# Streaming encoder step: new keys inside the cached keys' products, stick-breaking low halves on VectorE, and one rotary projection for all four query heads

## The chip, the cores and the metric

The kernel runs on one core of a Trainium2 chip. Each core has five engines with instruction streams of their own: PE (TensorE: matmuls and weight loads), DVE (VectorE), ACT (ScalarE), POOL (GpSimd) and SP (SyncE, which issues the DMAs here). They meet through semaphores. The metric is the time of one execution on the device in microseconds (us) (lower is better).

## The reference, cut to what matters

Two layers run over a prompt of 512 frames and over 8 running streams of 16 frames each (the sample, 128 rows in all). A layer projects its input, mixes it by three branches, and ends with an output projection, a layer norm, a squared-ReLU MLP and another layer norm. The change touches two branches: latent attention (MLA, 4 heads, with a rotary part of 64 per head) and stick-breaking attention (SB, 4 heads of 64).

```python
# both attentions of the sample see 1024 cached keys and 16 new ones of their own stream
ckv_all = jnp.concatenate([ckv_p, ckv], 1)
k_all   = jnp.concatenate([k_p, kc], 1)
# MLA
q = jnp.einsum('bsc,chd->bshd', rms_norm(b_cq, g_cq), w_uq)     # 384 -> 4 heads x (128 + 64)
q_rope = rope(q[..., NOPE_DIM:], q_pos)
scores = (einsum('bqhc,bkc->bhqk', q_lat, ckv) + einsum('bqhr,bkr->bhqk', q_rope, krope)) * MLA_SCALE
p = softmax(where(visible, scores, -inf)); out = einsum('bhqk,bkc->bqhc', p, ckv)
# SB
z = einsum('bqhd,bkhd->bhqk', q, k) * SB_SCALE
log_skip = where(mask, log_sigmoid(-z), 0)
w = where(mask, exp(log_sigmoid(z) + suffix_sum(log_skip)), 0); out = einsum('bhqk,bkhd->bqhd', w, v)
```

Everything is float32. The kernel splits each operand into a high part in the matmul's format (fp32r) and a low rest, and sums two or three products for each one of the reference.

## The kernel before, in words

Two streams of work are written as generators and woven together: P (the prompt) and S (the sample), whose steps of one layer are the preparation of queries and new keys (`s_prep`), the MLA over the caches (`lane_smla`), the SB over the caches (`lane_ssb`), and output and MLP (`s_out_mlp`). All instructions are recorded first; `Plan.schedule` then sets the order of every engine's instructions with a list scheduler (costs per instruction, tile slots, the rank of each instruction), and `Plan.follow` fixes that order. Every compute instruction is issued in one helper, so the profile shows them all at line 417 and all DMAs at line 433; they are told apart by the names of their tiles.

**Operands.** `split(hi, lo, src)` makes a high half with an ACT copy and a low half with a subtraction, on DVE unless an engine is given. For the caches of both attentions that engine is POOL (`KLO = VLO = pool`): tile `cT` holds a block of 512 cached keys (raw block `rawK`), `cN` a block of values (`rawV`).

**Scores of the sample** (`sample_scores`). The streams go in four pairs `pr`, two streams `j` each. For each stream there are two blocks `c` of 512 cached keys, each over two halves `ct` of the contraction, high and low: four matmuls of 512 columns into one PSUM bank (five in MLA, with the rotary part `kr`). The stationary operand holds high and low queries of 4 heads and 16 frames, so rows 64 to 127 of the result are added to rows 0 to 63 (`fold_to`: an ACT copy to `tmp`, a DVE addition). The new keys are a product of their own, `fresh`: four (MLA: five) matmuls of 128 columns, against the new keys of all 8 streams, of which a mask leaves 16. The banks are `x` (two) for SB and `sC` (three) for MLA and `fresh`.

**Values of the sample** (`weights_T`, `sample_values`). The 1152 weights of a pair (1024 cached, 128 new) are transposed in nine blocks of 128 to `pTs`, and are the stationary operands of matmuls with `cN`, 256 columns each; the ninth block multiplies the new values `cnh` or `vn`.

**Prompt's queries in MLA** (`lane_pmla`). The heads go in two pairs `a`, the frames in two halves `tp`. For each `(a, tp)`, `q_rope` projects the rotary part in 18 matmuls of 128 columns (bank `acc`, read `acc<-w,cqT`) and rotates it with five DVE instructions, and `q_nope` projects the rest in 18 matmuls of 256 columns (`acc<-cqT,w`). The weights come from `w_uq` in two loads for each `a`.

```python
            split(c4[:, 0], c4[:, 1], raw, KLO)
...
        def fresh(j, q, s_):
            for ct in range(2):
                pe.matmul(s_[:, :128], q[ct], new[:, 0, ct], start=(ct == 0), stop=False)
                pe.matmul(s_[:, :128], q[ct], new[:, 1, ct], start=False, stop=(ct == 1 and kr_new is None))
```

Of the kernel before, what the change touches and what calls it, by code (L numbers as in the profile page):

```python
# [20 lines left out]
L = 2  # L21
# [4 lines left out]
H = 4  # L26
# [70 lines left out]
class Plan:  # L97
# [111 lines left out]
    def schedule(self, prio):  # L209
# [32 lines left out]
        block = {name: len(v) for name, v in under.items()}  # L242
        opens = {}
# [42 lines left out]
        def issue(k, e, s):  # L286
# [18 lines left out]
            for name in o["tiles"]:  # L305
                left[name] -= 1
                if not left[name]:
# [9 lines left out]
                    grant(t)  # L317
            for x in succ[k]:
# [180 lines left out]
def hybrid_step(  # L499
# [5 lines left out]
    t_x, t_ckv, t_sbk, t_kr, t_ckvv, t_sbv, t_ws, t_wss, t_bs, t_bss, t_wukT, t_wkv, t_win, t_wout, t_wup,  # L505
# [27 lines left out]
    VLO = KLO = pool  # L533
# [123 lines left out]
    junk = cp.tile([128, 512], BF16, name="junk")  # L657

    def rms_to(out, src, g, n):
        ss = little([128, 1], F32, "ss")  # L660
        act.activation(junk[:, :n], src, AF.Square, accum_out=ss)
        r = rstd_of(ss, 1.0 / n, 1)
        dve.scalar_tensor_tensor(out, src, r[:, 0:1], g, ALU.mult, ALU.mult)
# [19 lines left out]
    def rope_apply(out, src, rope, t, pl, nh):  # L683
        t1 = pl.tile([128, nh, 64], F32, tag="rp1", name="rp1")
# [359 lines left out]
    def lane_pmla(l):  # L1044
# [5 lines left out]
        gmx = bcast(g_mix[l, 256:768], 512, mq, "gmxb")  # L1050
        W, KN, VM, CQ, CK, QR, QT, QX, PP = {}, {}, {}, {}, {}, {}, {}, {}, {}

        def q_tr(a, tp):

            if tp == 0:
                W[a] = load_wq(l, a), load_wkv(l, a, mp)
# [57 lines left out]
        def q_rope(a, tp):  # L1114
            cT, wq = CQ[a, tp], W[a][0]
            yield at("acc", cT, wq[2][1])
            pa = bank("acc")
            for i in range(2):
                c = slice(i * 128, (i + 1) * 128)
                o = pa[:, i * 128:(i + 1) * 128].rearrange("p (h d) -> p h d", h=2)  # L1120
                for k in range(3):
                    wh, wl = (x.rearrange("p (h d) -> p h d", h=2)[:, :, NOPE:] for x in wq[k])
                    mm3(o, cT[:, 0, k, c], cT[:, 1, k, c], wh, wl, k == 0, k == 2)
            qr = mp.tile([128, 4, 64], F32, tag="qr", name="qr")
            t = 2 * tp
            src = pa[:, :256].rearrange("p (t h d) -> p t h d", t=2, h=2)
            t2 = mp.tile([128, 4, 64], F32, tag="rp2", name="rp2")
            for i in range(2):
                hs = slice(2 * i, 2 * i + 2)
                cc = rope[:, 0, t + i].unsqueeze(1).to_broadcast([128, 2, 64])  # L1130
                ssn = rope[:, 1, t + i].rearrange("p (a b) -> p a b", a=2).unsqueeze(1).to_broadcast([128, 2, 2, 32])
                dve.tensor_tensor(qr[:, hs], src[:, i], cc, ALU.mult)
                sw = src[:, i].rearrange("p h (a b) -> p h a b", a=2)[:, :, ::-1, :]
                dve.tensor_tensor(t2[:, hs].rearrange("p h (a b) -> p h a b", a=2), sw, ssn, ALU.mult)
            dve.tensor_tensor(qr, qr, t2, ALU.add)
            qd = QR[a, tp] = mp.tile([128, 4, 2, 64], F32R, tag="d2", name="qd1")
            split(qd[:, :, 0], qd[:, :, 1], qr)

        def q_nope(a, tp):
            cT, wq = CQ.pop((a, tp)), W[a][0]  # L1140
            yield at("acc", cT)
            pa = bank("acc")
            for h in range(2):
                c = slice(h * 192, h * 192 + NOPE)
                for k in range(3):
                    mm3(pa[:, h * 256:(h + 1) * 256], wq[k][0][:, c], wq[k][1][:, c], cT[:, 0, k], cT[:, 1, k], k == 0, k == 2)
# [42 lines left out]
        late = []  # L1189

        def p_st(a, qt):
            nk = (qt + 1) * 128
            pp, r = PP.pop((a, qt))
# [14 lines left out]
        def p_v(a, qt, j, hs, pT, r):  # L1208
# [15 lines left out]
            if hs[-1] == 1:  # L1224
                if a == 1:
                    rms_to(xy[:, t, 512:1024], xy[:, t, 512:1024], gmx, 512)
# [199 lines left out]
    def weights_T(pl, p):  # L1426
        pTs = pl.tile([128, 9, 2, 2, 64], F32R, tag="pTs", name="pTs")
        for c0 in range(0, 9, 4):
            n = min(4, 9 - c0)
            yield at("sC", p)  # L1430
            pt = bank("sC")
            for i in range(n):
                tr(pt[:, i * 128:(i + 1) * 128], p[:, (c0 + i) * 128:(c0 + i + 1) * 128])
            split(pTs[:, c0:c0 + n, :, 0], pTs[:, c0:c0 + n, :, 1],
                  pt[:, :n * 128].rearrange("p (i j c) -> p i j c", j=2, c=64))
        return pTs

    def sample_scores(pl, s2, src, q_of, new, msk, n, kr_of=None, kr_new=None):
# [5 lines left out]
        def run(f):  # L1444
            return at("none" if f.args[3] else acc, *(x for x in f.args[4:] if x is not None))

        def block(j, q, c, ct, c4, kr):
            if ct == 0:
                held.append(bank(acc))
            s_ = held[0]  # L1450
            pe.matmul(s_, q[ct], c4[:, 0], start=(ct == 0), stop=False)
            pe.matmul(s_, q[ct], c4[:, 1], start=False, stop=(ct == 1 and kr is None))
            if ct:
                if kr is not None:
                    pe.matmul(s_, q[2], kr, start=False, stop=True)
                fold_to(s2[64 * j:64 * j + 64, 512 * c:512 * c + 512], held.pop(), 512, pl)

        def fresh(j, q, s_):
            for ct in range(2):
                pe.matmul(s_[:, :128], q[ct], new[:, 0, ct], start=(ct == 0), stop=False)  # L1460
# [441 lines left out]
```

## Time and profile before

| | |
|---|---|
| median of 3 runs | 1744.52 us (1735.86 to 1745.47) |
| the profiled execution's own time | 1738.5 us |
| its span, first to last instruction | 1736.6 us |
| instructions | 24320 |
| PE busy | 1665.9 us, 96% of the span, 8756 matmuls |
| DVE busy | 1167.8 us, 67% |
| ACT busy | 1017.5 us, 59% |
| POOL busy | 461.8 us, 27% |
| mean granted TensorE clock | 0.988 |
| DMA | 305.05 MB, mean 176 GB/s |

The profile is a page on one execution. A row such as `L417 PE MATMUL sC<-cT,qlT 128*128 128x512 f32 x128` reads: line 417, PE, bank `sC` written from moving operand `cT` and stationary operand `qlT`, array of 128 by 128, result of 128 partitions by 512 columns, 128 times. A matmul's shown duration holds its way through the array, so durations of neighbours overlap; what one costs in a dense stretch is read from start to start.

### The profile page before, as it was taken

Reading aid. Unit: us, or ns where it says so; the run is one execution under the profiler, and the core shown is the slowest. Engines: PE = TensorE matmul, PEld = TensorE weight load, DVE = VectorE, ACT = ScalarE, POOL = GpSimd, SP = SyncE. Lnnn points to the kernel's source line nnn. Section 1 sums busy time; section 2 is a strip of 40 time slices with the busy share of each in tenths; the row PEclk is TensorE's granted clock in tenths of the full one; section 3 lists DMA queues with packets and bytes.
Section 4 is the critical chain, followed back from the end, with each engine's and each line's share of the span. In section 5 each row is a group of like instructions: output and inputs, shape, how many; then the busy total and the mean of one; then the engine's idle time right before and its main releaser. Section 6 shows DMA issues by size and latency. Waiting matters only on the chain.

```text
span 1736.6 us, 24320 instructions
## 1 busy us (share of the span) xinstructions
PE 1665.9 (96%) x8756; PEld 1404.2 (81%) x8756; DVE 1167.8 (67%) x1592; ACT 1017.5 (59%) x1891; POOL 461.8 (27%) x320
## 2 busy tenths in 40 slices
PE   8999999899998999999999989999999999999998
PEld 6898988787886778888878988888778778788886
DVE  3487776846675587666744876868467766776766
ACT  4586785546664556463335857855467656564632
POOL 0000446534664300000000004466446552000000
PEclk9999999999999999999999999999999999999999
DMA  7236565445444587674353255665465456875732
GB/s 260 92 97 184 184 186 197 157 151 186 158 153 133 182 274 251 204 246 141 130 165 105 91 170 171 197 217 170 142 184 168 134 154 232 265 246 191 252 125 84
DMA packets 145817, 305.05 MB, mean 176 GB/s; under 512 B 32032, under 2 KB 46496, under 8 KB 145696
## 3 DMA queue, kind: packets, MB, share of 16 engines
q1 hardware_dynamic: 145696, 303.49, 54.2%
q8 instruction: 69, 1.13, 0.3%
q14 instruction: 52, 0.43, 0.1%
HBM read 286.14 MB, written 17.30 MB: 175 GB/s over the span
## 4 chain that ended last, share of the span: by engine, by line
PE 73%; ACT 8%; DVE 7%; DMA 7%; issue 4%; POOL 2%; SPq 0%; ACTq 0%; POOLq 0%; DVEq 0%
PE acc L417 52%; PE sC L417 11%; PE x L417 10%; DVE xy L417 2%; POOL cN L417 1%; DMA rawV<-in_t_ckvv_dram 1%; DMA rawK<-in_t_sbk_dram 1%; ACT w L417 1%; POOL cT L417 1%; DVE w L417 1%; ACT cN L417 1%; ACT cT L417 1%; DMA rawS<-in_w_up_dram 1%; DVE a L417 1%; DMA rawP<-in_w_down_dram 0%
## 5 line engine op out<-in xcount | busy, mean ns | idle before, releaser
L417 PE MATMUL acc<-yT,wx 128*128 128x512 f32 (+1 forms) x1632 | 398.2, 385 | 3.9 <-DVE yT L417 3.8
L417 PE MATMUL acc<-w,hT 128*128 128x512 f32 x1536 | 395.1, 398 | 2.3 <-DVE hT L417 1.7
L417 PEld LDWEIGHTS acc<-yT,wx 128*128 128x128 f32 x1632 | 291.8, 191 | 61.4 <-issue 3.9
L417 PEld LDWEIGHTS acc<-w,hT 128*128 128x128 f32 x1536 | 283.1, 189 | 65.5 <-DVE hT L417 2.1
L417 POOL TENSOR_TENSOR cT<-rawK,cT 128x512 fp32r<-128x512 f32 x128 | 200.8, 1575 | 164.2 <-ACT cT L417 120.3
L417 POOL TENSOR_TENSOR cN<-rawV,cN 128x512 fp32r<-128x512 f32 x128 | 195.1, 1532 | 168.6 <-ACT cN L417 164.5
L417 DVE TENSOR_TENSOR wS<-rawS,wS 128x1024 fp32r<-128x1024 f32 x144 | 175.0, 1223 | 82.9 <-ACT wS L417 82.7
L417 DVE TENSOR_TENSOR w<-rawP,w 128x1024 fp32r<-128x1024 f32 (+4 forms) x122 | 149.0, 1227 | 111.6 <-ACT w L417 110.0
L417 ACT CAST wS<-rawS 128x1024 fp32r<-128x1024 f32 x144 | 150.8, 1051 | 117.8 <-PE x L417 66.4
L417 PE MATMUL acc<-w,xT 128*128 128x512 f32 (+3 forms) x960 | 190.1, 353 | 2.2 <-ACT w L417 1.1
L417 PEld LDWEIGHTS acc<-w,xT 128*128 128x128 f32 x960 | 159.8, 193 | 20.5 <-ACT w L417 1.5
L417 ACT CAST w<-rawP 128x1024 fp32r<-128x1024 f32 (+4 forms) x122 | 122.5, 1006 | 73.3 <-DMA rawP<-in_w_down_dram 36.4
L417 DVE TENSOR_TENSOR xy<-xy,acc 128x512 f32<-128x512 f32 x128 | 86.6, 683 | 71.4 <-PE acc L417 70.8
L417 ACT CAST cN<-rawV 128x512 fp32r<-128x512 f32 x128 | 78.5, 620 | 66.0 <-DMA rawV<-in_t_sbv_dram 30.1
L417 PE MATMUL x<-cN,pTs 128*128 128x256 f32 x512 | 92.4, 290 | 11.5 <-ACT cN L417 5.8
L417 PEld LDWEIGHTS x<-cN,pTs 128*128 128x128 f32 x512 | 77.7, 190 | 30.3 <-ACT cN L417 11.8
L417 ACT CAST cT<-rawK 128x512 fp32r<-128x512 f32 x128 | 79.2, 620 | 36.4 <-PE sC L417 14.4
L417 PE MATMUL x<-wS,htS 128*128 128x512 f32 x384 | 99.5, 393 | 0.8 <-ACT htS L417 0.8
L417 PE MATMUL sC<-wS,x1TS 128*128 128x512 f32 x384 | 98.4, 394 | 0.0
L417 DVE TENSOR_TENSOR wx<-rawP,wx 128x1024 fp32r<-128x1024 f32 x68 | 85.9, 1265 | 12.6 <-ACT wx L417 11.9
L417 PEld LDWEIGHTS x<-wS,htS 128*128 128x128 f32 x384 | 72.0, 188 | 17.7 <-ACT htS L417 1.2
L417 PEld LDWEIGHTS sC<-wS,x1TS 128*128 128x128 f32 x384 | 71.8, 188 | 16.5 <-DVE wS L417 0.5
(277 smaller groups left out, 2635.2 us busy)
## 6 DMA issues: line engine op xcount, KB each, us to landing
rawP<-in_t_wup_dram SPq DMA_DIRECT2D x64, 512.0 KB, 4.0
rawP<-in_w_down_dram SPq DMA_DIRECT2D x64, 512.0 KB, 4.2
rawS<-in_w_up_dram SPq DMA_DIRECT2D x64, 512.0 KB, 4.6
rawS<-in_w_down_dram SPq DMA_DIRECT2D x64, 512.0 KB, 4.3
rawK<-in_t_ckv_dram SPq DMA_DIRECT2D x64, 256.0 KB, 3.0
rawV<-in_t_ckvv_dram SPq DMA_DIRECT2D x64, 256.0 KB, 3.1
rawK<-in_t_sbk_dram SPq DMA_DIRECT2D x64, 256.0 KB, 3.1
rawV<-in_t_sbv_dram SPq DMA_DIRECT2D x64, 256.0 KB, 3.0
```

The lines of the kernel that those rows point to most:

```text
L417: r = f(out, *a, **k)
```

## The change

1. **New keys.** `fresh` is gone from the scores. For `c = 1`, `cT` (and `kr`) become 544 columns wide: an ACT copy adds the 32 new keys of the pair, and the product goes into two banks of 272 columns each (for SB one `x` and one `sC`, for MLA two `sC`). The score tile shrinks from 1152 to 1056 columns, the mask from 224 to 32. The ninth block of weights is then 32 columns: one transposition to 32 partitions, at partitions `32 * pr` of `pTs`, and the two matmuls with the new values contract over these 32 partitions alone.
2. **Low halves.** `low_eng()` gives POOL in MLA over the caches and DVE elsewhere: in SB, the low halves of `cT` and `cN` move from POOL to DVE.
3. **Rotary queries.** For `a = 0`, `q_rope` projects all four heads: 18 matmuls of 256 columns for each `tp`, rotated by two calls of `rope_apply`; for `a = 1` only the split is left. The weights come laid out as `t_wq`, in three loads of 768 columns for each layer where there were four (768 and 384).
4. **Small.** The prompt's gain `gmx` is loaded at the first `p_st` of `a = 1` into the slot of `rope`; `junk` becomes one tile for each stream; the scheduler lets a tile's first instructions go only after the first instruction of the tile before it in the same slots (`begun`).

```diff
-    VLO = KLO = pool
+    def low_eng():
+        return pool if now["S"].startswith("smla") else dve
...
         def q_rope(a, tp):
-            cT, wq = CQ[a, tp], W[a][0]
...
-                    mm3(o, cT[:, 0, k, c], cT[:, 1, k, c], wh, wl, k == 0, k == 2)
...
+            if a == 0:
+                cT, (wh, wl) = CQ[a, tp], W["r"]
+                yield at("acc", cT, wl)
+                pa = bank("acc")
+                for i in range(2):
+                    c = slice(i * 128, (i + 1) * 128)
+                    for k in range(3):
+                        mm3(pa[:, i * 256:(i + 1) * 256], cT[:, 0, k, c], cT[:, 1, k, c], wh[:, k], wl[:, k], k == 0, k == 2)
+                qr = QA[tp] = mp.tile([128, 2, 4, 64], F32, tag="qr", name="qr", bufs=2)
+                src = pa.rearrange("p (t h d) -> p t h d", t=2, h=4)
+                for i in range(2):
+                    rope_apply(qr[:, i], src[:, i], rope, 2 * tp + i, mp, 4, qr[:, i])
...
-    def weights_T(pl, p):
+    def weights_T(pl, p, pr):
...
+        tr(pt[:32, :128], p[:, 1024:])
+        k = slice(32 * pr, 32 * pr + 32)
+        split(pTs[k, 8, :, 0], pTs[k, 8, :, 1], pt[:32, :128].rearrange("p (j c) -> p j c", j=2))
...
         def block(j, q, c, ct, c4, kr):
+            n = 272 if c else 512
             if ct == 0:
-                held.append(bank(acc))
-            s_ = held[0]
-            pe.matmul(s_, q[ct], c4[:, 0], start=(ct == 0), stop=False)
-            pe.matmul(s_, q[ct], c4[:, 1], start=False, stop=(ct == 1 and kr is None))
+                held.extend([bank(acc)] + ([bank("sC")] if c else []))
+            for e in range(2):
+                for i, s_ in enumerate(held):
+                    pe.matmul(s_[:, :n], q[ct], c4[:, e, i * n:i * n + n], start=(ct == 0 and e == 0), stop=(ct == e == 1 and kr is None))
...
-                    c4 = pl.tile([128, 2, 512], F32R, tag="cT", name="cT", bufs=2)
-                    split(c4[:, 0], c4[:, 1], raw, KLO)
+                    c4 = pl.tile([128, 2, 544], F32R, tag="cT", name="cT", bufs=2)
+                    split(c4[:, 0, :512], c4[:, 1, :512], raw, low_eng())
+                    if c:
+                        act.copy(c4[:, :, 512:], new[:, :, ct, 32 * pr:32 * pr + 32])
...
-            yield at("sC")
-            fresh(j, q, bank("sC"))
...
         def fresh(po, w, j, new):
-            pe.matmul(po[:, :256], w[8], new[:, 0], start=False, stop=False)
-            pe.matmul(po[:, :256], w[8], new[:, 1], start=False, stop=True)
+            k = slice(32 * pr, 32 * pr + 32)
+            pe.matmul(po[:, :256], w[8][k], new[k, 0], start=False, stop=False)
+            pe.matmul(po[:, :256], w[8][k], new[k, 1], start=False, stop=True)
...
-                    split(v[:, 0], v[:, 1], rv, VLO)
+                    split(v[:, 0], v[:, 1], rv, low_eng())
```

**PE, the first keys of the first SB lane** (layer 0; `x` and `sC` are banks, `acc` belongs to the prompt's MLP). Before:

```order
L417 MATMUL x<-cT,qS 128x512
L417 MATMUL sC<-knTs,qS 128x128 x4
L417 MATMUL acc<-yT,wx 128x512 x3
L417 MATMUL x<-cT,qS 128x512 x2
L417 MATMUL acc<-yT,wx 128x512 x7
L417 MATMUL x<-cT,qS 128x512
```

Now, its first block of `c = 1`:

```order
L433 MATMUL x<-cT,qS 128x272
L433 MATMUL sC<-cT,qS 128x272
L433 MATMUL acc<-w_6103,hT 128x512 x3
L433 MATMUL acc<-w_6183,hT 128x512
L433 MATMUL x<-cT,qS 128x272
L433 MATMUL sC<-cT,qS 128x272
L433 MATMUL x<-cT,qS 128x272
L433 MATMUL sC<-cT,qS 128x272
```

The four 128-column products with `knTs` are gone, and the block of 512 columns is two of 272, in turns into two banks.

**DVE, the same place.** Before:

```order
L417 TENSOR_TENSOR hT<-relu,hT 128x512
L417 TENSOR_TENSOR w_6201<-rawP,w_6201 128x1024
L417 TENSOR_TENSOR z<-x,tmp 64x512
L417 TENSOR_TENSOR wx<-rawP,wx 128x1024
L417 TENSOR_TENSOR z<-sC,tmp 64x128
L417 TENSOR_TENSOR relu<-relu 128x512
```

Now:

```order
L433 TENSOR_TENSOR hT<-relu,hT 128x512
L433 TENSOR_TENSOR z<-x,tmp 64x512
L433 TENSOR_TENSOR xy<-xy,acc 128x512 x2
L433 TENSOR_TENSOR cT<-rawK,cT 128x512 x2
L433 TENSOR_TENSOR cN<-rawV,cN 128x512 x2
L433 TENSOR_TENSOR z<-x,tmp 64x272
L433 TENSOR_TENSOR xy<-xy,acc 128x512
L433 TENSOR_TENSOR z<-sC,tmp 64x272
```

The low halves `cT` and `cN` of SB stand in DVE's queue among the prompt's evictions (`xy<-xy,acc`); in POOL's queue none of SB is left.

**PE, the first rotary queries of the prompt.** Before:

```order
L417 MATMUL acc<-w_1742,cqT 128x128 x6
L417 MATMUL acc<-w_1747,cqT 128x128 x3
L417 MATMUL acc<-w_1742,cqT 128x128 x6
L417 MATMUL acc<-w_1747,cqT 128x128 x3
L417 MATMUL acc<-ckT,w_1752 128x256 x12
```

Now:

```order
L433 MATMUL acc<-w_1738,cqT 128x256 x3
L433 MATMUL acc<-identr,kd_1841 128x128 x3
L433 MATMUL acc<-w_1738,cqT 128x256 x15
L433 MATMUL acc<-ckT,w_1748 128x256 x12
```

There are as many matmuls here, twice as wide; at `a = 1`, where 36 more stood in each layer, there are none now.

Over the whole program PE has 72 matmuls fewer, DVE 110 compute instructions more, ACT 78 more, POOL 128 fewer, and SP issues 2 DMAs fewer. The moved load of `gmx` was the 92nd row of SP's queue and is the 93rd. Of the 8684 matmuls left, 64 (the new values, in 32 pairs) take 32 rows of the array and 16 (the transpositions of new weights) take 32 columns; all others, like all before, take 128 by 128.

## Rows read from the trace of the kernel before

**Rows 1.** The page: span, busy shares, clock by slices, chain that ended last.

```profile
span 1736.6 us, 24320 instructions
PE 1665.9 (96%) x8756; PEld 1404.2 (81%) x8756; DVE 1167.8 (67%) x1592; ACT 1017.5 (59%) x1891; POOL 461.8 (27%) x320
...
PEclk9999999999999999999999999999999999999999
...
PE 73%; ACT 8%; DVE 7%; DMA 7%; issue 4%; POOL 2%; SPq 0%; ACTq 0%; POOLq 0%; DVEq 0%
```

**Rows 2.** Stretches of both SB lanes: length, busy time of each engine, clock, DMA.

```profile
407.00:600.00 193.00, 183.84 (x887) 149.84 (x888) 118.34 (x137) 116.14 (x197) 106.99 (x64) 0.98 0.48 153
1274.00:1452.00 178.00, 172.67 (x836) 139.86 (x837) 118.96 (x131) 109.87 (x183) 101.36 (x64) 1.00 0.50 157
```

**Rows 3.** Timeline of PE, first SB lane: start, length, instruction, how many merged.

```profile
407.76 0.56 PE L417 MATMUL sC<-knTs,qS 128*128 128x128 f32 x4
408.15 0.93 PE L417 MATMUL acc<-yT,wx 128*128 128x512 f32 x3
...
411.26 2.02 PE L417 MATMUL acc<-yT,wx 128*128 128x512 f32 x8
413.12 0.39 PE L417 MATMUL x<-cT,qS 128*128 128x512 f32 x1
```

**Rows 4.** Timeline of PE, the prompt's latent projections.

```profile
158.33 2.19 PE L417 MATMUL acc<-w,cqT 128*128 128x128 f32 x18
160.36 1.64 PE L417 MATMUL acc<-ckT,w 128*128 128x256 f32 x12
...
163.25 2.32 PE L417 MATMUL acc<-cqT,w 128*128 128x256 f32 x18
165.41 0.46 PE L417 MATMUL acc<-identr,qd 128*128 128x128 f32 x4
```

**Rows 5.** Timeline of PE, the input projection's 320 columns.

```profile
133.48 1.69 PE L417 MATMUL acc<-w,xS 128*128 128x320 f32 x10
135.00 2.51 PE L417 MATMUL acc<-w,xT 128*128 128x320 f32 x16
```

**Rows 6.** The tile of new values: duration in ns, least, median, most.

```profile
L417 PE MATMUL x<-vn,pTs x32: 278/281/287, 451.8 to 1450.5; 128*128 128x256 f32 x32
```

**Rows 7.** Timeline of PE, a transposition between matmuls.

```profile
569.52 1.31 PE L417 MATMUL acc<-w,hT 128*128 128x512 f32 x5
570.67 0.38 PE L417 MATMUL sC<-identr,o 128*128 128x128 f32 x2
570.89 1.04 PE L417 MATMUL sC<-identr,z 128*128 128x128 f32 x8
571.68 1.64 PE L417 MATMUL acc<-w,hT 128*128 128x512 f32 x6
```

**Rows 8.** POOL's groups, 425 to 590 us: busy us, mean ns, idle before.

```profile
L417 POOL TENSOR_TENSOR cN<-rawV,cN 128x512 fp32r<-128x512 f32 x30 | 48.9, 1640 | 44.0 <-ACT cN L417 43.9
L417 POOL TENSOR_TENSOR cT<-rawK,cT 128x512 fp32r<-128x512 f32 x26 | 46.3, 1790 | 28.4 <-ACT cT L417 28.4
```

**Rows 9.** One DVE group, 425 to 590 us (POOL busy), then 640 to 800 (POOL idle).

```profile
L417 DVE TENSOR_TENSOR relu<-relu 128x512 f32<-128x512 f32 x9 | 9.2, 1019 | 6.9 <-ACT relu L417 6.9
...
L417 DVE TENSOR_TENSOR relu<-relu 128x512 f32<-128x512 f32 x8 | 5.5, 685 | 0.0
```

**Rows 10.** PE's waits, 425 to 590 us: total us, times, longest.

```profile
PE x L417 <- POOL cN L417: 4.9, 1, 4.9
```

**Rows 11.** Groups of the whole span that the change's small parts are like.

```profile
L417 DVE TENSOR_TENSOR o<-x,tmp 64x256 f32<-64x256 f32 x32 | 13.3, 416 | 34.7 <-ACT tmp L417 34.3
L417 ACT COPY ycT<-sC 64x32 f32<-64x32 f32 x32 | 5.8, 181 | 4.2 <-PE sC L417 3.7
```

**Rows 12.** Stretches of 100 us, columns as in rows 2.

```profile
500.00:600.00 100.00, 91.53 (x454) 74.61 (x453) 54.09 (x62) 54.23 (x96) 46.67 (x28) 0.97 0.43 135
...
1100.00:1200.00 100.00, 95.03 (x533) 81.12 (x533) 78.14 (x116) 66.18 (x142) 70.20 (x45) 0.98 0.61 195
```

More of the change, by code (lines that the diff above doesn't have):

```diff
@@ L242, in schedule @@
         block = {name: len(v) for name, v in under.items()}
+        begun = [set() for _ in range(n)]
+        for p, t in tags:
+            for a, b in zip(t["names"], t["names"][1:]):
+                mine = self.tiles[b]["ops"]
+                for k in mine:
+                    if not ops[k]["deps"] & mine:
+                        begun[min(self.tiles[a]["ops"])].add(k)
+        for ks in begun:
+            for k in ks:
+                need[k] += 1
         opens = {}
@@ L317, in issue @@
                     grant(t)
+            for x in begun[k]:
+                ready[x] = max(ready[x], s)
+                need[x] -= 1
+                if not need[x] and x not in glued:
+                    loose(x)
             for x in succ[k]:
@@ L1114, in q_rope @@
         def q_rope(a, tp):
-            cT, wq = CQ[a, tp], W[a][0]
[L1116 to L1122, printed above, removed]
-                    mm3(o, cT[:, 0, k, c], cT[:, 1, k, c], wh, wl, k == 0, k == 2)
@@ L1124, in q_rope @@
[L1124 to L1134, printed above, removed]
@@ L1187, in s_st @@
             PP[a, qt] = pp, lr
-        late = []
+        late, gmx = [], []
         def p_st(a, qt):
             nk = (qt + 1) * 128
+            if a and not gmx:
+                gmx.append(bcast(g_mix[l, 256:768], 512, mp, "rope"))
             pp, r = PP.pop((a, qt))
@@ L1444, in run @@
         def run(f):
[L1445 removed]
+            return at("none" if f.args[3] else acc, *(x for x in f.args[4:6] if x is not None))
         def block(j, q, c, ct, c4, kr):
+            n = 272 if c else 512
             if ct == 0:
[L1449 to L1452 removed]
+                held.extend([bank(acc)] + ([bank("sC")] if c else []))
+            for e in range(2):
+                for i, s_ in enumerate(held):
+                    pe.matmul(s_[:, :n], q[ct], c4[:, e, i * n:i * n + n], start=(ct == 0 and e == 0), stop=(ct == e == 1 and kr is None))
             if ct:
[L1454 to L1460, printed above, removed]
[L1461 to L1464 removed]
+                for i, s_ in enumerate(held):
+                    if kr is not None:
+                        pe.matmul(s_[:, :n], q[2], kr[:, i * n:i * n + n], start=False, stop=True)
+                    fold_to(s2[64 * j:64 * j + 64, 512 * c + i * n:512 * c + i * n + n], s_, n, pl)
+                held.clear()
         for j in range(2):
@@ L1572, in q_of @@
                 return [x[:, 2 * pr + j].rearrange("p a h q -> p (a h q)") for x in (qlT[:, 0], qlT[:, 1], qrS)]
-            yield from sample_scores(smp, s2, keys(pr), q_of, cnT, msk[:, 96 - 32 * pr:224 - 32 * pr], KV["smla"][0], kr_of, krN)
+            yield from sample_scores(smp, s2, keys(pr), q_of, cnT, msk, KV["smla"][0], pr, kr_of, krN)
         def mid(pr):
@@ L1583, in back @@
             s2, r = st.pop(pr)
-            pTs = yield from weights_T(smp, s2)
+            pTs = yield from weights_T(smp, s2, pr)
             used[0] += 1
@@ L1594, in done @@
                          pf[:, :256].rearrange("p (c x) -> p c x", c=2))
-            yield from sample_values(smp, pTs, values(pr), cnh, done, KV["smla"][1])
+            yield from sample_values(smp, pTs, values(pr), cnh, done, KV["smla"][1], pr)
         yield from pipeline(front, mid, back, 4)
@@ L1830, in _constants @@
     mask[:, 1] = np.where(p[None, :] // 64 <= p[:, None] // 64, 0, neg)
-    x = np.arange(224)
-    same = x[None, :] // QS == 6 + p[:, None] // 64
-    wide = np.zeros((128, 2, 224), np.float32)
+    x = np.arange(32)
+    same = x[None, :] // QS == p[:, None] // 64
+    wide = np.zeros((128, 2, 32), np.float32)
     wide[:, 0] = np.where(same, 0, neg)
@@ L1868, in _laid_out @@
     out["t_wkv"] = rows(both, 0, 2, 5, 1, 4, 3, 6).reshape(L, 2, 128, 1024)
+    q = g["w_uq"].reshape(L, 3, 128, H, NOPE + ROPE)
+    parts = [q[..., NOPE:], q[:, :, :, :2, :NOPE], q[:, :, :, 2:, :NOPE]]
+    out["t_wq"] = np.stack([rows(x, 0, 2, 1, 3, 4).reshape(L, 128, 768) for x in parts], 1)
     cuts = [O_U, O_CQ, O_CKV, O_C, O_C + 512, O_C + 768]
```

76 lines of the change are left out of this document (38 added, 38 removed).

## The prediction

> **What bounds the kernel now.** I read the page first, then stretches of time, then the timeline of PE. The page [rows 1] shows one engine that is nearly always at work: PE is busy 96% of the span, no other engine over 67%, and PE is 73% of the chain that ended last. The clock row holds 9 in every slice, so no slice runs at the lower level throughout. The stretches of both stick-breaking (SB) lanes [rows 2] say the same of the place where the change does most: in 193 and 178 us PE is busy 183.8 and 172.7, together 356.5 of 371 (96%); DVE 118.3 and 119.0 (64%), ACT 61%, POOL 56%. In such a stretch a microsecond taken off PE's queue is close to a microsecond off the time, and a microsecond put on DVE costs nothing until PE waits for it. So the sum is made on PE's queue first, and then on what PE would wait for.
>
> A matmul's shown length overlaps its neighbours, so the cost is taken from start to start. 512 columns: eight from 411.26 to 413.12, 0.2325 us each; 128 columns in the scores: four from 407.76 to 408.15, 0.0975 each [rows 3]. 128 columns in the rotary projection: 18 from 158.33 to 160.36, 0.113 each; 256 columns: 18 from 163.25 to 165.41, 0.120 each [rows 4]. So 128 and 256 columns cost nearly the same, which is the lever of parts 1 and 3: narrow matmuls are paid as wide ones. 320 columns: ten from 133.48 to 135.00, 0.152 each [rows 5].
>
> **Part 1, new keys.** For each pair, stream and layer, four (SB) and five (MLA) products of 512 columns and as many of 128 become twice as many of 272. That is 4 pairs x 2 streams x 9 x 2 layers = 144 of each kind removed: 144 x (0.2325 + 0.0975) = 47.5 us. Added are 288 of 272 columns. No row has 272; it lies a quarter of the way from 256 to 320, so 0.120 + 0.008 = 0.128 (bounds 0.120 and 0.152), 36.9 us. Net **-10.6 us** of PE (bounds -13 and -4).
>
> The new values and the last weights now use a part of the array: 32 pairs of matmuls over 32 rows and 16 transpositions to 32 columns, 48 places that PE enters and leaves, 96 edges. Their own columns cost as before. Before, every matmul is 128 by 128, so no row shows such an edge. Below, it costs nothing: where PE goes from five matmuls to two transpositions, eight more and back [rows 7], starts stay 0.10 to 0.11 us apart and the next matmul follows at once, so a change of kind and shape is free. Above, PE lets each matmul run out before the next starts: a 256-column one takes 281 ns [rows 6] and costs 120 in a dense run, so 0.161 us an edge, 15.5 in all. I take a third of that, 0.05 us, **+5 us**, nearer the end that the closer row shows. The Trainium skill speaks against the change here: TensorEngine Tiling (Array Packing), section Tiling Modes, says that changing the tiling mode drains TensorE. No run here shows it; by that rule the term would be 15.5 and not 5, and it stands below as a rival.
>
> ACT gets 80 copies of 32 new keys (0.181 us each by the nearest row [rows 11], 14.5 us) and folds of 272 columns in place of 512 and 128. These lie in ACT's idle 39% [rows 2], each between a block's high half and its product, while the low half, at 0.69 us or more on either engine, is still under way: nothing. If that cover went, all 80 would cost 14.5. DVE's folds (two near 0.416 us [rows 11]) replace one longer and one shorter; scans, softmax and mask lose 8% of their columns. In the noise of this sum: nothing.
>
> **Part 2, low halves.** POOL loses 128 subtractions, 1.64 and 1.79 us each in SB [rows 8]. PE waited for one of them visibly, 4.9 us at once [rows 10]; that goes: **-4.9 us**. DVE gets 128 of the same shape. Without POOL such an instruction takes 0.685 us on DVE, and 1.019 while POOL works beside it [rows 9]; POOL is now idle in these lanes, so 128 x 0.685 = 87.7 us, less what its neighbours no longer lose to POOL. The relu squares alone lose 9 x 0.33 = 3 us in 165; with the other two-input instructions I estimate 10 in both lanes. DVE goes from 237 to about 315 of 371 us, 85%. That is the new risk: the low halves stand in one queue with the prompt's evictions, weight splits and the long scans of the same lane, and both the bank `acc` and the next block wait for that queue. Below, PE waits no more than now (0). Above, its share falls from 96% to the 91.5% of the worst stretch of [rows 12], 371 x 0.045 = 17 us. The other stretch there has DVE at 78% and PE at 95%, one point under the SB lanes: 371 x 0.01 = **+4 us**, which I take.
>
> **Part 3, rotary queries.** 144 matmuls of 128 columns become 72 of 256: 144 x 0.113 = 16.2 us, 72 x 0.120 = 8.6 us, **-7.6 us** of PE. The rotation does the same columns in fewer DVE instructions, off the path. What goes too is cover: at `a = 1` PE had 18 such matmuls (2.0 us) between transpositions and the key products, twice in a layer. If nothing of the sample stands ready, up to 8 us of the saving comes back as waits. The sample's lane is under way there, so I take nothing.
>
> **Part 4.** Three weight loads for four, and a gain loaded one row later in SP's queue: it waits for the last reader of `rope`, long before `p_st` needs it, and queued behind it are the sample's cache loads, which would come late only if that reader did. Nothing. The scheduler's new condition moves instructions everywhere; no row prices it (rival 3).
>
> **Sum:** -10.6 + 5 - 4.9 + 4 - 7.6 = **-14 us**. Against the profiled execution's own 1738.5 (span 1736.6) that is 1724.5. The median of the runs is 1744.5, 6 us above the profiled one, with runs from 1736 to 1745; the forecast is told against the median: **1730 us**, -0.8%.
>
> **Forecast (chance 0.48): 1716 to 1736.** PE's work falls by the 18 us of parts 1 and 3, and edges and new waits take back a part.
>
> **Rival 1, the edges drain PE (0.20).** PE stays the bound but pays 0.16 us at each of 96 edges: -14 + 10.5 = -3.5, 1741, no change to be measured. For it: a matmul's way through the array is 161 ns longer than its cost. Against it: [rows 7].
>
> **Rival 2, slower (0.13): DVE comes late in SB.** Each of the 128 low halves stands behind other work, and PE's block waits for it with the prompt's banks waiting too. One that comes a DVE instruction late costs 0.685. The 23 us that the other terms give (-10.6 - 7.6 - 4.9) are gone at 34 late ones; with 64, half of them, it is 44 - 23 + 5 = +26, 1770. For it: 85% of one queue in order. Against it: PE has the prompt's matmuls to do meanwhile.
>
> **Rival 3, the new order does better (0.10).** PE's whole idle time in the SB lanes is 14.5 us [rows 2]. If it goes with POOL, not 4.9 but 14.5, and no new wait comes: -18.2 - 14.5 + 5 = -28, 1717 and down to 1706.
>
> **Rival 4, the change doesn't do what it says (0.09).** PE's queue gets shorter, but the new order spends it as waits elsewhere: the lost cover of part 3 (8 us) and about as much in the other stages. 1740 to 1748.
>
> **How the numbers follow.** 1711 to 1748 holds the forecast, rivals 1 and 4 and half of rival 3, 0.82. About 0.5% (8.7 us) is what a measurement of this kernel tells from no change. Faster than 1735.8: nearly all of the forecast, rival 3, a little of rival 1, 0.61. Slower than 1753.2: rival 2 for the most part, 0.12. Between: 0.27.
>
> **What would show it.** In the changed profile, 272 columns should cost 0.12 to 0.13 us from start to start, no matmul `sC<-knTs` or `sC<-cnT` is left, and POOL is empty in SB. An edge is right at 0.05 if the pair `x<-vn` starts within 0.17 us of the matmul before it, and rival 1 is right if PE starts 0.25 us or more apart there. DVE in SB should be near 85%, its low halves near 0.69, and PE's share there no lower than 94%; under 92%, with waits for DVE's `cT`, `cN` or `xy`, rival 2 is right. The prediction is wrong if PE's summed matmul time doesn't fall by some 18 us, or falls and the span doesn't.

## The result, and the profile after

The change takes 1728.74 us (median of 8 runs) where the kernel before takes 1739.36 in the same session: ratio 0.9923, 95% interval 0.9904 to 0.9943. (One of the eight runs took 4124 us and is left out of the ratio.) That is faster by 0.8%, and 1730 us, also 0.8% less, was forecast. The forecast was told against 1744.5 us, the median of three runs of the kernel before; with eight runs that median is 1739.4, so the two ratios are what to compare. The profiled execution took 1729.99 us, its span is 1728.2. The forecast's sum holds as a total; the sections below show that the gain of part 2 was far undersized, that the edges cost PE's queue more than twice their term, and that one edit costed at nothing costs 10 us when it stands alone.

The page of the change, beside [rows 1]:

```profile
span 1728.2 us, 24196 instructions
PE 1661.9 (96%) x8684; PEld 1397.6 (81%) x8684; DVE 1204.0 (70%) x1702; ACT 1022.4 (59%) x1969; POOL 246.6 (14%) x192
...
PEclk9998999899999999999999989999999999999999
...
PE 74%; DVE 8%; DMA 7%; ACT 6%; issue 2%; POOL 1%; SPq 0%; ACTq 0%; POOLq 0%; DVEq 0%
```

POOL loses 215 us of work, and DVE gains 36, not the 88 us that 128 low halves of 0.685 us would bring. PE has 72 matmuls fewer, yet is busy only 4 us less. Both are read below. First the two SB lanes, with columns as in [rows 2]:

```profile
421.00:595.00 174.00, 173.00 (x849) 140.53 (x847) 139.01 (x196) 113.25 (x208) 0.00 (x0) 1.00 0.53 169
1276.00:1455.00 179.00, 176.42 (x858) 142.21 (x859) 139.85 (x198) 115.17 (x211) 0.00 (x0) 1.00 0.53 166
```

PE is busy 349.4 of 353 us (99%) and idle 3.6. In the kernel before, the same lanes (407 to 603 and 1274 to 1460 us) hold 382 us with PE busy 367.3, idle 14.7. POOL is empty there, as said. DVE is at 278.9 of 353 (79%), not 85%. DVE's groups in the first lane (busy us, mean ns, idle before) answer to [rows 9]:

```profile
L433 DVE TENSOR_TENSOR cT<-rawK,cT 128x512 fp32r<-128x512 f32 x32 | 21.9, 686 | 3.9 <-ACT cT L433 3.7
L433 DVE TENSOR_TENSOR cN<-rawV,cN 128x512 fp32r<-128x512 f32 x32 | 21.6, 686 | 4.8 <-ACT cN L433 4.5
...
L433 DVE TENSOR_TENSOR relu<-relu 128x512 f32<-128x512 f32 x11 | 7.5, 686 | 2.1 <-ACT relu L433 1.9
```

The low halves take 0.686 us on DVE as forecast, and the relu squares, 1.019 beside POOL, now take the same 0.686.

The rotary queries, timeline of PE: 18 matmuls of 256 columns, 0.122 from start to start ((2.35 - 0.28) / 17), as forecast from [rows 4].

```profile
175.34 2.35 PE L433 MATMUL acc<-w,cqT 128*128 128x256 f32 x18
```

And one place where the new values enter PE's queue, in the first SB lane, PE and then its weight loads:

```profile
511.99 0.64 PE L433 MATMUL x<-cN,pTs 128*128 128x256 f32 x4
512.56 0.50 PE L433 MATMUL x<-vn,pTs 32*128 32x256 f32 x2
512.99 0.73 PE L433 MATMUL acc<-yT,wx 128*128 128x512 f32 x2
513.55 0.29 PE L433 MATMUL x<-cT,qS 128*128 128x272 f32 x1
513.68 0.29 PE L433 MATMUL sC<-cT,qS 128*128 128x272 f32 x1
513.80 0.29 PE L433 MATMUL x<-cT,qS 128*128 128x272 f32 x1
513.93 0.29 PE L433 MATMUL sC<-cT,qS 128*128 128x272 f32 x1
514.06 0.40 PE L433 MATMUL acc<-yT,wx 128*128 128x512 f32 x1
...
511.76 0.66 PEld L433 LDWEIGHTS x<-cN,pTs 128*128 128x128 f32 x4
512.56 0.29 PEld L433 LDWEIGHTS x<-vn,pTs 32*128 32x128 f32 x2
512.99 0.30 PEld L433 LDWEIGHTS acc<-yT,wx 128*128 128x128 f32 x2
```

272 columns: four from 513.55 to 514.06, 0.1275 us each; 0.128 was forecast. The transposition to 32 columns costs no more than one to 128: from the start of a last transposition, over the 512-column matmul behind it, to the next start it is 0.344 us in the median for either. But the weights for the first `vn` start to load at 512.56, together with their own matmul, where those for `cN` start 0.23 us ahead of theirs; and so with the weights behind the pair. The second `vn`'s weights start 0.107 us after the first `vn` did, which is 0.115 us ahead of their own matmul. Over the 32 pairs the medians from start to start are 0.209 us into the pair (0.119 in a dense run), 0.222 between its two, 0.205 out of it, and the 512-column matmul behind takes 0.337 (0.230 before): 0.09 + 0.10 + 0.09 + 0.11 = 0.39 us a pair, some **12 us** of PE's queue in all. So PE's work fell by the forecast 18 us, and 12 came back here.

### The profile page after: what moved, and what is told of

Its sections match the earlier page's. It is cut to its first block, busy times and chain, and to the rows that moved or that the text cites. A ratio compares the mean times of both kernels' runs of the same rounds, so it can differ in the third digit from the quotient of the medians.

```text
span 1728.2 us, 24196 instructions
## 1 busy us (share of the span) xinstructions
PE 1661.9 (96%) x8684; PEld 1397.6 (81%) x8684; DVE 1204.0 (70%) x1702; ACT 1022.4 (59%) x1969; POOL 246.6 (14%) x192
## 4 chain that ended last, share of the span: by engine, by line
PE 74%; DVE 8%; DMA 7%; ACT 6%; issue 2%; POOL 1%; SPq 0%; ACTq 0%; POOLq 0%; DVEq 0%
PE acc L433 54%; PE sC L433 11%; PE x L433 10%; DVE xy L433 2%; DMA rawK<-in_t_sbk_dram 1%; DVE w L433 1%; DMA rawV<-in_t_ckvv_dram 1%; DMA krs<-in_t_kr_dram 1%; ACT cT L433 1%; ACT w L433 1%; DMA rawV<-in_t_sbv_dram 1%; POOL cN L433 1%; DMA rawS<-in_w_down_dram 1%; ACT cN L433 1%; DMA rawS<-in_w_up_dram 1%
## 5 line engine op out<-in xcount | busy, mean ns | idle before, releaser
L433 DVE TENSOR_TENSOR w<-rawP,w 128x1024 fp32r<-128x1024 f32 (+3 forms) x120 | 143.8, 1202 | 96.7 <-ACT w L433 96.2
L433 PE MATMUL acc<-w,xT 128*128 128x512 f32 (+3 forms) x960 | 195.4, 359 | 8.1 <-DVE ev L433 5.7
L433 ACT CAST w<-rawP 128x1024 fp32r<-128x1024 f32 (+3 forms) x120 | 121.8, 1016 | 73.2 <-DMA rawP<-in_w_down_dram 36.3
L433 POOL TENSOR_TENSOR cT<-rawK,cT 128x512 fp32r<-128x512 f32 x64 | 92.4, 1450 | 119.4 <-ACT cT L433 101.0
L433 POOL TENSOR_TENSOR cN<-rawV,cN 128x512 fp32r<-128x512 f32 x64 | 91.2, 1433 | 85.1 <-ACT cN L433 67.1
```

The costliest lines, as they stand in the source:

```text
L433: r = f(out, *a, **k)
```

## The experiments

Two questions: what do the 32-row matmuls cost in the end, and which part carries the gain? Each ratio is to the kernel before in the same session. **Theory A**: partial rows expose the weight loads. Its rivals: an emptied PE at a change of form alone, or no cost at all because PE waits there anyway. **Theory B**, formed on the way: part 2 carries the gain, and parts 1 and 3 little. The first two kernels below leave out the right weights for the new values and take those of another block, so they answer for time alone.

### 32, 64 or 128 rows in the same order

```diff
-            k = slice(32 * pr, 32 * pr + 32)
-            pe.matmul(po[:, :256], w[8][k], new[k, 0], start=False, stop=False)
-            pe.matmul(po[:, :256], w[8][k], new[k, 1], start=False, stop=True)
+            pe.matmul(po[:, :256], w[7], new[:, 0], start=False, stop=False)
+            pe.matmul(po[:, :256], w[7], new[:, 1], start=False, stop=True)
```

> The change, but the 64 matmuls with the new values contract over all 128 rows (weights of the last cached block and new values of all streams) in place of 32; every engine's order stays as it is. The new values' part of the result is not the reference's. Theory A (in the trace of the change a pair of 32-row matmuls costs 0.09 us on entry, 0.10 between its two, 0.09 and 0.11 behind it, 0.39 in all, 32 pairs): 12 us less than the change, about 1716 us, ratio to before near 0.985, and starts around `vn` and `cnh` 0.12 us apart. The forecast's own price of an edge (0.05 us, 64 edges): 3 us less, 1725.5. Rival (PE is not what counts there, another wait takes the place): no difference, 1729.

Measured: 1722.71 us, ratio 0.9885 (0.9863 to 0.9907), span 1720.9. The same place as above, PE and weight loads:

```profile
508.42 0.64 PE L433 MATMUL x<-cN,pTs 128*128 128x256 f32 x4
508.89 0.40 PE L433 MATMUL x<-vn,pTs 128*128 128x256 f32 x2
509.14 0.62 PE L433 MATMUL acc<-yT,wx 128*128 128x512 f32 x2
509.60 0.29 PE L433 MATMUL x<-cT,qS 128*128 128x272 f32 x1
...
508.78 0.31 PEld L433 LDWEIGHTS x<-vn,pTs 128*128 128x128 f32 x2
```

From the first `cN` to the first `cT` it is 1.18 us, not 1.56, with the same instructions in the same order: 0.38 a pair, as theory A says. The weights load 0.11 us ahead of their matmul. But the ratio falls by 0.0038, 6.6 us, and the span by 7.3: about half of the 12 us on PE's queue came out at the end. PE is busy 10.6 us less than in the change (1651.3 after 1661.9) and idle 3.4 us more, so a part went where the forecast's rivals put such savings, into waits. The expectation of 0.985 was missed. The two ratios' intervals just overlap; the run with 64 rows, which follows, gives a closer comparison.

The 64-row form, with `k = slice(64 * (pr // 2), 64 * (pr // 2) + 64)` and `w[7][k]`:

> As the run before it, but the same 64 matmuls contract over 64 rows (a half of the last cached block's weights); every engine's order as in the change, and the new values' part of the result is again not the reference's. Theory A1 (any part of the rows makes PE load weights only when the matmul before has gone through): as the change, 1729 us, and pairs at 0.21 to 0.23 us from start to start. Theory A2 (it is the quarter of the array, or how far apart the row groups lie): 1716 to 1723.

Measured: 0.9904 (0.9882 to 0.9925), span 1724.7; into, within and out of a pair 0.209, 0.223 and 0.206 us, as with 32 rows:

```profile
L433 PEld LDWEIGHTS x<-vn,pTs x32: 182/184/186, 459.2 to 1438.7; 64*128 64x128 f32 x32
L433 PE MATMUL x<-vn,pTs x32: 275/329/383, 459.2 to 1438.9; 64*128 64x256 f32 x32
```

A1 holds on PE's queue. The total lies between the two others, within their intervals, though the queue costs the same as in the change. Against this run, full rows are worth 0.0019, 3.3 us, and 3.8 us of span: so 3 to 7 us, with an uncertainty as large. The Trainium skill, TensorEngine Tiling (Array Packing), section Tiling Modes, says that a change of the tiling mode drains TensorE; 0.209 us in place of 0.119 at the entry agrees in direction. The second matmul of a pair changes no mode and pays as much, which that rule does not give. TensorE: Matmul & The Clock Gate, Part 3, says in its list of what overlaps that weight loads overlap matmuls in flight only where the row groups differ. For pairs in one group of 32 or 64 rows the trace agrees (0.107 us from the first matmul's start to the second's load); for the 128-row form it does not, since there a load starts 0.11 us ahead of its matmul, while a matmul on the same rows streams. (A sentence further up in the same part lets a load run ahead into a background weight buffer too, which would fit that form.)

### Full rows, with zeros in the others

First with a tile `pN` of 128 rows for the last weights, and POOL's memset put into the planned order:

```diff
+        pool.memset(r32(pN), 0.0)
...
-        split(pTs[k, 8, :, 0], pTs[k, 8, :, 1], pt[:32, :128].rearrange("p (j c) -> p j c", j=2))
+        split(pN[k, :, 0], pN[k, :, 1], pt[:32, :128].rearrange("p (j c) -> p j c", j=2))
...
+            pe.matmul(po[:, :256], w[8], new[:, 0], start=False, stop=False)
+            pe.matmul(po[:, :256], w[8], new[:, 1], start=False, stop=True)
```

> The change with the last weights in a tile of 128 rows, set to zero by POOL for each pair before the 32 rows are written; the 64 matmuls contract over all 128 rows; result as the reference's. Theory A: 12 us less than the change, 1716 us (ratio 0.985 to before), give or take some 5 us for an order that the scheduler makes anew; the 16 memsets on POOL (some 0.3 us each by POOL's rate on like shapes) cost PE nothing. The forecast's price of an edge: 1725. Rival: POOL's memset comes late for the last weights in MLA, where POOL is busy, PE waits, 1729 or more.

Measured: 1726.94 us, 0.9906 (0.9883 to 0.9928): hardly better than the change, and 11 us above theory A's 1716. The scheduler had made a new order, so this left open whether memset or order took the gain. The last run of the study set the ninth block of `pTs` to zero outside the plan, with the matmuls over 128 rows as in the last diff, which leaves the order alone:

```diff
         pTs = pl.tile([128, 9, 2, 2, 64], F32R, tag="pTs", name="pTs")
+        nc.gpsimd.memset(r32(pTs[:, 8]), 0.0)
```

> The change with the 64 matmuls of the new values over all 128 rows; the ninth block of `pTs` is set to zero by POOL for each pair before its 32 rows are written, and, unlike the first try of this, every engine's order is the change's own, with only 16 memsets between. Result as the reference's. Theory A with what the run over another block showed (PE's queue 11 us shorter, a part of it turned into waits): ratio to before 0.9885, 1722 us, 3 to 9 us under the change and about level with part 2 alone. If the memsets hold up POOL's low halves in MLA: 0.991 and more, as the first try.

Measured: 1723.45 us, 0.9894 (0.9860 to 0.9927), span 1723.1. So full rows measure some 5 us under the change here, memset included, but the two intervals overlap: the price on PE's queue is shown, what of it comes out in the time is 3 to 7 us and not settled.

### One part at a time

The scheduler's condition alone:

```diff
+        begun = [set() for _ in range(n)]
...
+            for x in begun[k]:
+                ready[x] = max(ready[x], s)
+                need[x] -= 1
...
```

> The kernel before with the scheduler's new condition (`begun`) and nothing else: the same work in a new order. Theory (the gain is work off PE and POOL off the SB lanes): ratio to before 1.000, within 0.004 either way for the order. Rival 3 (the new order does better): 0.995 or less. This is also the base for the three runs behind it, which have the condition too.

Measured: 1752.98 us, **1.0057** (1.0033 to 1.0081), above the expectation. Alone, the condition costs 10 us by its order. Rival 3 had the sign wrong.

Part 2 with the condition:

```diff
-                    split(c4[:, 0], c4[:, 1], raw, KLO)
+                    split(c4[:, 0], c4[:, 1], raw, low_eng())
...
-                    split(v[:, 0], v[:, 1], rv, VLO)
+                    split(v[:, 0], v[:, 1], rv, low_eng())
```

> The kernel before with part 2 (SB's low halves on DVE) and the condition. Theory from the trace of the change (PE's waits in the two SB lanes fall from 16 to 5 us once POOL is out): 9 to 11 us less than with the condition alone, ratio to it 0.994. The forecast's own two terms (-4.9 + 4): 0.999 to 1.000. Rival 2 (DVE late): over 1.003.

Measured: 1726.86 us, **0.9920** (0.9890 to 0.9949): with neither new keys nor rotary queries as fast as the whole change, and 24 us under its base, more than any of the three expectations. Without the condition:

> The kernel before with part 2 alone (SB's low halves of cT and cN on DVE), without the scheduler's condition. Theory B (part 2 carries the gain, since POOL's slow low halves held PE in the SB lanes; the condition alone costs some 0.6%): ratio to before 0.986 to 0.988, about 1720 us, better than the change. If the run of part 2 with the condition owed its time to a lucky order: 0.992 or more. The forecast's two terms for part 2 (-4.9 + 4): 0.9995.

Measured: 1723.85 us, **0.9898** (0.9868 to 0.9927), between the two expectations, 18 us under the kernel before. Beside part 2 the condition costs 4 us (0.9920 against 0.9898, intervals overlapping), not 10, so the parts do not simply add up. Its SB lanes and its page:

```profile
414.00:588.00 174.00, 171.10 (x837) 137.55 (x836) 139.38 (x194) 112.54 (x191) 0.00 (x0) 1.00 0.54 171
1263.00:1442.00 179.00, 175.16 (x856) 142.06 (x857) 142.21 (x197) 115.39 (x195) 0.00 (x0) 1.00 0.54 169
...
PE 1659.2 (97%) x8756; PEld 1397.7 (81%) x8756; DVE 1209.6 (70%) x1720; ACT 1016.8 (59%) x1891; POOL 252.5 (15%) x192
```

PE's idle time in the two lanes is 6.7 us, against 14.7 before, with all 8756 matmuls still there. Taken out of the change instead:

```diff
-        return pool if now["S"].startswith("smla") else dve
+        return pool
```

> The change with SB's low halves back on POOL, all else as in the change. Theory B (part 2 carries the gain; parts 1 and 3 give PE 20 us less work and spend most of it on 32-row pairs and waits): ratio to before 1.002 to 1.006, and PE's waits over 0.15 us in the two SB lanes back from 5 to 16 us or more. The forecast (-0.9 us for part 2): 0.993, about as the change.

Measured: 1741.87 us, 1.0007 (0.9988 to 1.0026), a little under theory B's range: part 2 is worth 0.0084, 15 us, within the change. Its SB lanes, then groups of POOL and DVE in the first, then two groups of PE's waits, the longest of the first lane and the only one for POOL in the second:

```profile
412.00:611.00 199.00, 192.57 (x924) 154.88 (x923) 130.94 (x145) 121.51 (x217) 103.62 (x64) 0.99 0.50 160
1280.00:1464.00 184.00, 177.29 (x858) 143.34 (x858) 115.80 (x134) 115.72 (x212) 98.91 (x64) 0.99 0.53 165
...
L433 POOL TENSOR_TENSOR cN<-rawV,cN 128x512 fp32r<-128x512 f32 x32 | 54.3, 1707 | 52.1 <-ACT cN L433 52.1
...
L433 DVE TENSOR_TENSOR xy<-xy,acc 128x512 f32<-128x512 f32 x26 | 17.5, 683 | 13.0 <-PE acc L433 12.9
...
L433 DVE TENSOR_TENSOR relu<-relu 128x512 f32<-128x512 f32 x14 | 14.6, 1045 | 5.5 <-ACT relu L433 5.4
...
PE x L433 <- ACT cT L433: 3.0, 4, 1.5
...
PE x L433 <- POOL cN L433: 1.4, 2, 1.0
```

PE is idle 13.1 us again (383 less 369.9), relu is back at 1.045 us. Theory B holds on three comparisons: 15, 18 and 24 us. DVE's busy time over the whole program is 1166.5 us here and 1204.0 in the change: 128 low halves of 0.686 us (87.8) raise it by 37.5 only, so POOL's had cost DVE's other instructions 50 us. The Trainium skill, SBUF — State Buffer, section SBUF: two separate sides, gives a reason: a GpSimd instruction and one of VectorE with two inputs in SBUF hold a shared port pair exclusively, each for its whole length. The durations agree: `relu`, with both inputs in SBUF, falls from 1.045 to 0.686 us, while `xy<-xy,acc`, with one input in PSUM, takes 0.683 in both runs. No run here looks at the port itself.

How POOL's work reached PE is less clear. In this run PE's visible waits in the two lanes are 13.9 us, 9.9 behind ACT, 2.6 behind DVE and only 1.4 behind POOL. Whether ACT came late through stretched DVE instructions or through tiles that POOL gave back late, no run separates. The 4.9 us of the kernel before [rows 10] can be followed further back:

```profile
533.25 6.79 POOL L417 TENSOR_TENSOR cN<-rawV,cN 128x512 fp32r<-128x512 f32 x1 [10.14 <-ACT cN L417]
...
533.39 2.54 DVE L417 TENSOR_TENSOR_SCAN a<-a 128x1152 f32<-128x1152 f32 x1
535.85 0.66 DVE L417 TENSOR_TENSOR hT<-relu,hT 128x512 fp32r<-128x512 f32 x1
536.44 1.34 DVE L417 TENSOR_TENSOR z<-z,a 128x1152 f32<-128x1152 f32 x1
537.70 1.21 DVE L417 TENSOR_TENSOR wx<-rawP,wx 128x1024 fp32r<-128x1024 f32 x1
...
540.09 1.22 PE L417 MATMUL x<-cN,pTs 128*128 128x256 f32 x4 [4.86 <-POOL cN L417]
```

POOL's subtraction, 1.30 us in the median of that lane, took 6.79 here: it ended 1.1 us after a row of DVE instructions without a pause between them. So the longest wait put down to POOL was one in which POOL itself was held up beside DVE.

The new keys with the condition, on the kernel before, low halves on POOL:

```diff
-                    c4 = pl.tile([128, 2, 512], F32R, tag="cT", name="cT", bufs=2)
+                    c4 = pl.tile([128, 2, 544], F32R, tag="cT", name="cT", bufs=2)
...
-            yield at("sC")
-            fresh(j, q, bank("sC"))
```

> The kernel before with part 1 (new keys in the products of 272 columns, 32-row matmuls for the new values) and the condition; low halves on POOL in both lanes, rotary queries as before. PE's dense work falls by 13 us (144 x (0.231 + 0.11) removed, 288 x 0.125 added). The forecast (edges 5 us in all): ratio to the run with the condition alone 0.996. If the 32-row pairs cost their whole 12 us in the span: 0.999 to 1.000.

Measured: 1813.12 us, **1.0410** (1.0378 to 1.0441), far above every expectation. Stretches, ACT and PE of the first MLA lane:

```profile
266.00:370.00 104.00, 72.97 (x253) 52.06 (x251) 28.17 (x58) 54.99 (x119) 66.33 (x53) 0.61 0.49 151
...
368.35 0.60 ACT L433 ACTIVATE junk<-sC 128x512 bf16<-128x512 f32 x1 [2.50 <-PE sC L433]
...
369.44 0.63 ACT L433 ACTIVATE junk<-xy 128x512 bf16<-128x512 f32 x1
...
264.99 0.60 PE L433 MATMUL acc<-identr,xy 128*128 128x128 f32 x4
...
373.13 1.07 PE L433 MATMUL acc<-identr,xy 128*128 128x128 f32 x4
```

From 265.3 to 373.1 us no matmul of the prompt (`acc`) runs: 108 us in which PE has the sample's chain alone, is busy 73 of 104 us, and is granted 0.61, between the two levels of 1.2 and 2.4 GHz (at the lower one a 512-column `cT` shows 0.79 us). It ends when the prompt's `junk<-xy` goes, right behind the sample's `junk<-sC`, the last step of its lane. Both write squares into one scratch tile. So theory C, and the one edit of part 4 that it names:

```diff
-    junk = cp.tile([128, 512], BF16, name="junk")
+    junk = {k: cp.tile([128, 512], BF16, name="junk" + k) for k in "PS"}
...
-        act.activation(junk[:, :n], src, AF.Square, accum_out=ss)
+        act.activation(junk[now["by"]][:, :n], src, AF.Square, accum_out=ss)
```

> The run with the keys alone (1.041, the prompt's matmuls stand still for 108 us of the first MLA lane), with one thing of part 4 added: `junk`, the scratch tile into which both streams write squares that nobody reads, becomes one tile for each stream. Theory C (the prompt stood still because its write to `junk` was ordered behind the sample's, which comes at the end of its lane): the gap is gone and the ratio falls to 1.000 to 1.003, that is the condition's 0.6% less some 6 us for the keys. Rival (the products of 272 columns or the 32-row matmuls starve PE in that lane): the ratio stays over 1.03 and the gap stays.

Measured: 1752.18 us, **1.0055** (1.0033 to 1.0076), and no gap of `acc` over 7.2 us is left. Theory C is shown, though the ratio is a little above its range; 62 us hung on a tile that nobody reads. The shared tile alone doesn't do it: the run with the condition alone has one `junk` too, and its longest stretch without `acc` is 6.7 us. It takes an order that puts the prompt's write behind the sample's last one. The run also tells what the keys with their pairs are worth: 1.0055 against the condition's 1.0057, nothing that can be told from zero, with an uncertainty of some 5 us.

Parts 3 and 4 with the condition, on the kernel before (`q_rope` and `q_nope` as in the change):

```diff
-                W[a] = load_wq(l, a), load_wkv(l, a, mp)
+                if a == 0:
+                    W["r"] = load_w(t_wq[l, 0].rearrange("p (k c) -> p k c", c=256), 3, 256)
+                W[a] = load_w(t_wq[l, 1 + a].rearrange("p (k c) -> p k c", c=256), 3, 256), load_wkv(l, a, mp)
```

> The kernel before with parts 3 and 4 (rotary queries of all four heads at once, weights laid out for it, the gain loaded later) and the condition. The forecast (7.6 us of PE's queue, no cover lost): ratio to the run with the condition alone 0.9956. Rival 4 (the cover lost at a = 1): 0.999 to 1.000. If the 15 us by which undoing this part slowed the change belong to the part and not to a new order: 0.991.

Measured: 1809.20 us, **1.0387** (1.0354 to 1.0420), far above every expectation again, with two stretches like the one above:

```profile
343.00:393.00 50.00, 31.97 (x110) 24.15 (x109) 9.19 (x17) 19.29 (x35) 23.40 (x18) 0.53 0.40 125
1244.00:1288.00 44.00, 25.96 (x92) 19.87 (x92) 11.46 (x17) 18.83 (x34) 19.25 (x15) 0.58 0.42 131
...
392.42 0.62 ACT L433 CAST wuv<-rawV 128x512 fp32r<-128x512 f32 x1 [2.12 <-DMA rawV<-in_t_wkv_dram]
393.07 1.27 ACT L433 ACTIVATE relu<-acc,bup 128x512 f32<-128x512 f32 x2
```

`junk` is already two tiles here. The prompt's MLP starts with `relu<-acc` only when the sample's values are through. By the addresses that the kernel gives its tiles, `relu` (up to byte 155520 of a partition) lies on the memory of the sample's `cN` in MLA (from 155168) in this version: the second scratch tile has moved `relu` up by 1024 bytes. In the change, whose score tiles and masks are smaller, `cN` starts at 155936, and in the kernel before `relu` ends at 154496, so there they don't meet. That is argued from addresses and trace; no run moved the tile. So this run does not price the rotary part. Taking it out of the change does, from the other side (the last diff the other way round, the gain's later load left in):

> The change with the prompt's rotary queries as before (36 matmuls of 128 columns for each a in a layer, weights in four loads). The forecast's term (7.6 us of PE's queue): 1736 us, ratio to before 0.997. Rival 4 (the cover lost at a = 1 gives the saving back as waits): 1729, no difference to the change. A new order may add some 5 us either way.

Measured: 1744.85 us, 1.0011 (0.9995 to 1.0028): 0.0088 slower than the change, 15 us, twice the term, in another order, and above both expectations. The run with the low halves back on POOL has the condition, keys, two scratch tiles and the rotary part; the one with keys and two scratch tiles lacks the rotary part and the gain's later load: 1.0007 against 1.0055, 8 us. So 8 to 15.

## Why the prediction was right, and where it was not

Four runs lead from the kernel before to the change, a part at a time: condition 1.0057; and keys with two scratch tiles 1.0055; and rotary part 1.0007; and low halves 0.9923. In us: +10, 0, -8, -15, together -13. Each step has an uncertainty of some 5 us and a new order, and another sequence of parts would give other steps (the condition costs 4 us beside part 2). Against the forecast's steps:

- **Keys, -10.6.** Right on the queue: no `sC<-knTs` or `sC<-cnT` is left, and 272 columns cost 0.1275 us.
- **Edges, +5 at 0.05 each.** Mis-sized: 0.39 us a pair, 12 us on PE's queue, because four starts around a pair are late, and not only its two edges. On that queue the keys' net is then -10.6 + 12, near nothing, and nothing was measured, where the forecast had -5.6. The forecast looked at five matmuls beside transpositions [rows 7], where the array stays whole; that row says nothing on a part of it. Rival 1 was near in size (15.5) but not in its cause: 0.21 us at the entry lies between its 0.25 and the forecast's 0.17, the second of the pair pays too, and the transpositions pay nothing. In the time, 3 to 7 of the 12 us come out when the rows are full.
- **Low halves, -4.9 and +4.** The step that failed most: -0.9 us net was forecast, 15 to 24 us of gain were measured. The one visible wait for `cN` [rows 10] was taken for all that POOL cost, and DVE's load was reckoned with 10 us of relief for its neighbours where 50 came. So DVE stood at 79%, PE's waits for DVE's `cT` in the SB lanes are 0.4 us in all, and rival 2 (DVE late) has nothing for it. Rival 3's other half came true: PE's idle time there fell from 14.7 to 3.6 us, through POOL and not through the order. Of the 15 us, 9.5 are this idle time (13.1 to 3.6). Over the whole program the two profiled spans differ by 12.5 us, 8.6 of PE's idle time and 3.9 of its busy time for the same matmuls. The lanes' clock goes with the latter: 1.00 in the change, 0.99 with POOL at work (0.62 from 488 to 492 us, 0.67 from 1358 to 1362). No run separates idle time from clock.
- **Rotary, -7.6.** Right: 0.122 us for 256 columns, 8 us by one comparison, 15 by the other. A lost cover as large as 8 us isn't seen. No run has this part alone in an order without a stall.
- **Part 4, nothing.** Wrong twice. The condition costs 10 us alone. The scratch tiles, costed at nothing, kept the prompt running in the run of the keys: without them it stood 108 us. The change without them was not run.
- **The named test** that PE's summed time falls by 18 us fails as put: busy fell by 4.0 us (1665.9 to 1661.9), since a matmul that waits for its weights shows as busy (`x<-vn`, 281 ns in the median before [rows 6], shows 328), and 12 us of that came in. With full rows it is 1651.3, 14.6 below the kernel before. The dense prices are as forecast.

So the total came out at 1729 for 1730 because an undersized gain (part 2, by 14 us) met undersized costs (keys with their pairs by 6, condition by 10). That the errors cancelled is luck; the prices of single matmuls and the gain of part 3 were foreseen, the gain's main source was not. Two versions measure below the change, part 2 alone with 0.9898 and the change with full rows with 0.9894; both intervals overlap the change's.

## What to carry to other kernels

Before shrinking a contraction to the rows that matter, look whether the weights still load under the matmul before: full rows with zeros cost the same columns and keep the stream dense. When pricing a move off POOL, count the stretched instructions of its neighbours too, and not the visible waits alone. And where a planner sets the order, a part tried by itself can meet a stall that has nothing to do with it (a shared scratch tile, a reused address): look for a stretch in which one stream has no matmul before giving the time to the edit.

## What was not expected of the hardware

- Matmuls over 32 and over 64 rows, and the first 128-row one behind them, load their weights later than in a dense run of 128 rows: 0.209 us from start to start into a pair, 0.222 within it and 0.205 out of it, against 0.119, the same for both sizes.
- A part of the columns costs nothing where a part of the rows does: a last transposition to 32 columns and the 512-column matmul behind it take 0.344 us from start to start, as with 128 columns.
- The low halves of SB on POOL lengthened DVE's instructions with two inputs in SBUF (`relu` from 0.686 to 1.045 us, 50 us in all over the program), not those with one input in PSUM; and one on POOL took 6.79 us in place of 1.30 beside a row of DVE instructions.
- With the prompt absent, PE was granted a mean clock of 0.53 to 0.61 over stretches of 44 to 104 us, in which it was busy 59 to 70% of the time.
